# A hybrid attention trunk on one core: another order of layer 0's attention pairs, other stretches of dense work between them, and a second tile for transposed probabilities

## The chip, the cores and the metric

The kernel runs on one core of a Trainium2 chip. The metric is the device time of one execution in microseconds (us), the median of several runs. The engines are TensorE (PE in the profile; its weight loads, which can lie beside its matmuls, are PEld), VectorE (DVE), ScalarE (ACT), GpSimd (POOL) and SyncE (SP, which issues nearly all transfers).

## What is computed

The reference is a decoder trunk of two residual layers, with 512 tokens and a model width of 1024, in float32. Each layer is `x = x + mixer(rmsnorm(x))`, then `x = x + conv_glu_ffn(rmsnorm(x))`. Layer 0's mixer has two groups of eight heads of width 64 that share one input and one output projection:

```python
o_sb = stick_breaking_attention(q, k, v)        # 8 heads
o_nsa = nsa_attention(...)                      # 8 heads, 2 groups of K and V, 3 gated branches
return concatenate([o_sb, o_nsa]) @ w_out
```

A stick-breaking head has `a = exp(log_sigmoid(z) + after)`, where `after` is the sum of `log_sigmoid(-z)` over all later keys up to the query: a running sum along the keys, and no division. A sparse (NSA) head adds three softmax branches, each times its gate: over 31 compressed blocks of keys, over selected blocks, and over a window. With 512 tokens the selected branch and the window branch are plain causal attentions with K and V of their own. Layer 1's mixer has 16 heads of softmax attention with a learned decay.

## The kernel before

**Precision and dense work.** A float32 product with weights is made of three matmuls: activations and weights are both split into a high and a low part (`XH`, `XL`; `whi`, `wlo`), and high by high, high by low and low by high are added up in PSUM. `weights()` (line 177) loads a weight tile and makes its parts, one cast on ACT and one subtraction on DVE. `unit()` (line 197) is one projection of 128 columns: 8 steps of 3 matmuls of 512 columns. `vgroup()` (line 210) projects V for four heads (16 steps of 6 narrower matmuls), `proj()` (line 473) is a part of the output projection (4 steps in layer 0, since each half of the heads has its own), `compress()` (line 640) makes the compressed keys or values out of what `c_use()` (line 619) has gathered, and `mid()` (line 755) loads x again. All weights, and the swapped rows of the rotary helper `rope()` (line 518), are loaded by SP, one after the other. These are generators; `Fill` (line 35) holds them in one queue and `step(n)` runs n steps of it, `get()` runs steps until a named result is there.

**Attention.** Two heads at a time are a pair (`Pair`, line 358; `SbPair`, line 441). A pair has these parts: `S((3,))`, `S((2,))`, `S((0, 1))` make the scores of query blocks 3, 2, and 0 with 1, in PSUM, and start the softmax (DVE, ACT) or the stick-breaking chain (ACT: abs, exp, ln; DVE: one combined operation, the running sums of line 462, the subtraction of line 463; ACT: exp). `N` scales by the denominator and the gate on POOL (softmax pairs alone). `T(0)` to `T(4)` transpose the probabilities, four 128 by 128 blocks at a time, into one PSUM bank; each is copied by ACT into the tile `ph` (line 426). `V` multiplies by the values, 16 matmuls, into the bank `o`, which is then copied out (line 470). `Cmp` (line 691) is the compressed branch; its `S` and `T` hang on the first pair of two heads, as `extra`. Score tiles have two buffers of two banks each, the bank for transposes and the bank `o` have one each, and `ph` has one buffer.

**Order.** `pipeline()` (line 71) takes one pair per turn: the scores of the newest pair, the transposes of the one before it, and `V` of the one before that. A turn is a list of up to ten parts, and after each part a tenth of the turn's dense steps is run:

```python
seq: S(3)+S(2) | V | T(0) | N(2) | T(1) | S(0,1) | T(2) | N(0) | T(3) | T(4)
pairs = [four SbPair] + [h for p in range(4) for h in nsa_pairs(p)]
pipeline(pairs, fl, lambda n: 28 if n < 4 else 6)
```

So layer 0 (line 495) has first four stick-breaking turns with 28 dense steps each, then eight sparse turns (selected and window branch of four pairs of heads) with 6 steps each, and two turns without scores. The dense queue of layer 0 has 163 steps. Layer 1 (line 822) calls the same `pipeline()` with eight pairs and 22 steps a turn. The order in which an engine gets its instructions is fixed when the program is built: the order of the calls is the priority, and an instruction that is planned to have its inputs late lets others of its engine go first. On the chip every engine then takes them in that fixed order.

**Last steps of layer 0.** The output projection's first half (`part`, line 752) needs the outputs of pairs 0 to 3 and goes into the dense queue; the second half (line 763) needs all pairs and comes last, followed by the next norm.

Of the kernel before, what the change touches and what calls it, by code (L numbers as in the profile page):

```python
# [9 lines left out]
F32 = mybir.dt.float32  # L10
# [7 lines left out]
P = 128  # L18
# [13 lines left out]
NPERM = [0, 4, 1, 5, 2, 6, 3, 7]  # L32

# [37 lines left out]
def pipeline(pairs, fill, steps):  # L71

    p1 = p2 = None
    for n, h in enumerate(list(pairs) + [None, None]):
        seq = []
        if h is not None:
            seq.append(lambda: (h.S((3,)), h.S((2,))))
        if p2 is not None:
            seq.append(p2.V)
        if p1 is not None:  # L80
            seq.append(lambda: p1.T(0))
        if h is not None:
            seq.append(lambda: h.N(2))
        if p1 is not None:
            seq.append(lambda: p1.T(1))
        if h is not None:
            seq.append(lambda: h.S((0, 1)))
        if p1 is not None:
            seq.append(lambda: p1.T(2))
        if h is not None:  # L90
            seq.append(lambda: h.N(0))
        if p1 is not None:
            seq += [lambda: p1.T(3), lambda: p1.T(4)]
        f = steps(n)
        done = 0
        for m, a in enumerate(seq):
            a()
            want = f * (m + 1) // len(seq)
            fill.step(want - done)
            done = want  # L100
        p2, p1 = p1, h
# [3 lines left out]
def trunk(ctx, tc, A):  # L105
# [51 lines left out]
    maskb = cp.tile([P, 2, 2, P], BF, name="maskb")  # L157
# [5 lines left out]
    def load_consts():  # L163
        for t, n in ((ones, "ones"), (ident, "ident"), (mask32, "mask2"), (mk, "mk"), (conv, "conv")):
            sp.dma_start(t, A[n])
        pool.tensor_copy(maskb, mask32)

    def warm():

        z = cp.tile([P, SEQ], BF, name="zero")  # L170
# [95 lines left out]
    def finish(fp, src, oh, ol):  # L266
# [20 lines left out]
        def square(m, b, ps):  # L287

            t, w = parts[b], width[b]
            added.append(dve.tensor_add(X[m][:, t], X[m][:, t], ps[:, 0:w]).ins)  # L290
            sq = wp.tile([P, SEQ], F32, tag="sq2", bufs=4, name="sq")
            act.activation(sq[:, 0:w], X[m][:, t], AF.Square)
            return sq[:, 0:w]
# [64 lines left out]
    class Pair:  # L358

# [32 lines left out]
        def S(self, ii):  # L392
            ps = self.scores(ii, None)
            for i in reversed(ii):
                w = P * (i + 1)
                o = EOFF[i] - EOFF[ii[0]]
                for hd in range(2):
                    ei = self.e[:, hd, EOFF[i]:EOFF[i] + w]
                    nm, dn = self.nm[:, hd, i:i + 1], self.dn[:, hd, i:i + 1]
                    add = mk[:, 384 - P * i:512] if self.bias is None else self.bias[:, hd, EOFF[i]:EOFF[i] + w]  # L400
                    dve.tensor_tensor_reduce(ei, ps[:, hd, o:o + w], add, scale=-1.0, scalar=3.0e38,  # L401
                                             op0=ALU.add, op1=ALU.min, accum_out=nm)
                    act.activation(ei, ei, AF.Exp, bias=nm, scale=-1.0, accum_out=dn)  # L403
            if self.extra is not None and 0 in ii:
                self.extra.S()
# [12 lines left out]
        def T(self, n):  # L418
            if n == 0:
                self.ph = self.ap.tile([P, 2560], F32, tag="ph", bufs=1, name="ph")  # L420
            ps = pp.tile([P, SEQ], F32, tag="t", bufs=1, name="t")
            for hd, j in TGRP[n]:
                for i in range(j, NB):
                    o = POFF[hd][j] - 512 * n + (i - j) * P
                    pe.transpose(ps[:, o:o + P], self.e[:, hd, EOFF[i] + j * P:EOFF[i] + j * P + P], ident)  # L425
            act.copy(self.ph[:, 512 * n:512 * n + 512], ps)  # L426
            if self.extra is not None and n == 4:
                self.extra.T()
# [12 lines left out]
    class SbPair(Pair):  # L441


        def S(self, ii):
            def more(ps, r, i):
                for n in range(2):
                    mm(ps[:, i * P:i * P + P], maskb[r, 0, n], maskb[r, 1, n], False, n == 1)
# [47 lines left out]
    def layer0():  # L495
        with ExitStack() as es:
# [8 lines left out]
            def o_tiles(c):  # L505

                if c >= 4 and c % 2 == 0:
# [10 lines left out]
            def rope(f):  # L518
# [5 lines left out]
                u = ap.tile([P, SEQ], F32, tag="rp", bufs=1, name="rp")  # L524
                dve.tensor_mul(u, s, rs)
                dve.tensor_mul(f, f, rc)
                dve.tensor_add(f, f, u)
# [9 lines left out]
            def k_use(key, rp):  # L537
                def use(ps):
                    f = evac(qp, ps, 1.0, "k", 3)
# [5 lines left out]
            def v_use(key, j):  # L545
                def use(tb, ps):
# [4 lines left out]
                    act.activation(gates[:, tb, 8 * j:8 * j + 8], ps[:, 256:264], AF.Exp, scale=nrt[:, tb:tb + 1])  # L551
                    if tb == NB - 1:
                        VT[key] = VT["new"]
                return use
# [38 lines left out]
            def early_bank():  # L593

                if not early:
# [5 lines left out]
                   vgroup(wv(0), 264, v_use(0, 0), v_sp))  # L601
            fl._start(2)
            load_consts()
# [15 lines left out]
            def c_use(key):  # L619
                def use(ps):  # L620
                    f = evac(qp, ps, 1.0, "k", 3)
# [105 lines left out]
            def nsa_pairs(p):  # L727
# [10 lines left out]
                for b, key in ((1, "s"), (2, "w")):  # L738
# [10 lines left out]
            pairs = [SbPair(ap, lambda p=p: fl.get(Q, p), lambda p=p: fl.get(K, p), lambda p=p: fl.get(VT, p // 2),  # L749
                            2 * (p % 2), new_o, True, True, done=pair_done(p)) for p in range(4)]  # L750
            pairs += [h for p in range(4) for h in nsa_pairs(p)]
            part = lambda m: proj(m, [(A["wo0"][m][:, 0:4], 4)], OH[:4], OL[:4], ready=lambda: 3 in OF)
            nq = lambda p: unit(U[8 + p], q_use(("n", p), True))

            def mid():
                make_gates()
# [3 lines left out]
            fl.add(nq(1), mid(), part(0), part(1), nq(2), part(2), part(3), nq(3), part(4), part(5), part(6), part(7))  # L760
            pipeline(pairs, fl, lambda n: 28 if n < 4 else 6)
# [233 lines left out]
def layout(inp):  # L995
# [11 lines left out]
    for n, v in enumerate((sv[:, :256], sv[:, 256:], np.concatenate([vsl, vwn], 1))):  # L1007
        a[f"wv0_{n}"] = _vg(np.concatenate([v, g[:, 8 * n:8 * n + 8]], 1))
    wo = i["ev_w_out"][0].reshape(16, 64, D)
    a["wo0"] = _units(wo[list(range(8)) + [8 + h for h in NPERM]].reshape(D, D))  # L1010
# [32 lines left out]
```

## Time and profile before

| | us |
|---|---|
| median of 3 runs | 1291.14 |
| lowest and highest run | 1289.74, 1291.53 |
| the profiled execution | 1291.93 |
| its span, first to last instruction | 1290.1 |
| TensorE busy in the span | 1271.2 (99%) |
| weight loads busy | 1002.1 (78%) |
| VectorE, ScalarE, GpSimd busy | 693.7, 555.7, 147.9 |

The profile is that of one execution. Matmuls are pipelined and their ends are modelled, so a TensorE that is shown busy need not be at its peak: a start that comes late is often counted to the instruction before it. The chain that ended last is followed back from the last instruction to what released each; a piece of it lasts from its start to that of the next.

### The profile page before, as it was taken

To read this page: it belongs to the slowest core of one execution; us is meant where nothing else is said; L and a number is where in the kernel's file an instruction comes from. 1 tells how busy PE (TensorE), PEld (TensorE's weight loads), DVE (VectorE), ACT (ScalarE), POOL (GpSimd) and SP (SyncE) were. 2 spreads that over 40 slices of the span, in tenths; PEclk is the share of its full clock that TensorE was granted. 3 is DMA by queue.
4 is the path that set the end of the run, shared out by engine and by line. 5 is a ranking of instruction groups with operands and counts; after the bars stand their busy time and mean duration, and the time that the engine had idled before them with its cause. 6 is when DMAs were issued, how large, how long until landed. Compare 5 with 4: busy or idle time off the path is not lost.

```text
span 1290.1 us, 16521 instructions
## 1 busy us (share of the span) xinstructions
PE 1271.2 (99%) x6338; PEld 1002.1 (78%) x6338; DVE 693.7 (54%) x1142; ACT 555.7 (43%) x948; POOL 147.9 (11%) x206
## 2 busy tenths in 40 slices
PE   8999999999999999999999999999999999999997
PEld 5876856567888888888888877866788888888886
DVE  7468665538655434565443443344755543556534
ACT  6556465645433223334342554444533322333442
POOL 0000042223000000000111433321200000000010
PEclk9999999999999999999999999999999999999999
DMA  6315201003333233232344453411333223333232
GB/s 224 95 59 147 87 21 42 19 26 123 98 99 94 78 106 107 92 98 89 94 127 141 145 151 92 120 51 51 122 98 98 88 90 100 108 94 94 88 99 90
DMA packets 50639, 124.00 MB, mean 96 GB/s; under 512 B 6320, under 2 KB 15792, under 8 KB 50560
## 3 DMA queue, kind: packets, MB, share of 16 engines
q1 hardware_dynamic: 49040, 121.35, 31.0%
q10 hardware_dynamic: 1520, 1.59, 0.4%
q8 instruction: 50, 0.82, 0.3%
q14 instruction: 29, 0.24, 0.1%
HBM read 119.28 MB, written 2.13 MB: 94 GB/s over the span
## 4 chain that ended last, share of the span: by engine, by line
PE 93%; DVE 3%; ACT 2%; issue 1%; DMA 1%; SPq 0%; DVEq 0%; ACTq 0%
PE mm L115 80%; PE s L115 6%; PE o L115 4%; PE t L425 3%; DVE e L462 1%; DVE wlo L194 0%; ACT whi L193 0%; DMA x<-x 0%; ACT xh L248 0%; DMA wraw<-wu 0%; DVE lt L457 0%; DVE acc L239 0%; ACT lt L454 0%; DVE e L463 0%; DVE e L401 0%
## 5 line engine op out<-in xcount | busy, mean ns | idle before, releaser
L115 PE MATMUL mm<-xh,whi 128*128 128x512 f32 x936 | 372.2, 398 | 0.9 <-ACT xh L248 0.6
L115 PE MATMUL mm<-xh,wlo 128*128 128x512 f32 x936 | 365.1, 390 | 1.6 <-DVE wlo L194 1.6
L115 PE MATMUL mm<-xl,whi 128*128 128x512 f32 x936 | 365.5, 391 | 0.1
L193 ACT CAST whi<-wraw 128x1024 fp32r<-128x1024 f32 (+2 forms) x219 | 200.0, 914 | 383.5 <-PE mm L115 362.7
L194 DVE TENSOR_TENSOR wlo<-wraw,whi 128x1024 fp32r<-128x1024 f32 (+2 forms) x219 | 236.4, 1079 | 137.4 <-ACT whi L193 134.7
L115 PEld LDWEIGHTS mm<-xh,whi 128*128 128x128 f32 x936 | 175.8, 188 | 44.8 <-issue 8.8
L115 PEld LDWEIGHTS mm<-xl,whi 128*128 128x128 f32 x936 | 175.8, 188 | 40.0 <-DVE xl L249 1.8
L115 PEld LDWEIGHTS mm<-xh,wlo 128*128 128x128 f32 x936 | 176.1, 188 | 37.0 <-DVE wlo L194 2.2
L115 PE MATMUL mm<-gh,whi 128*128 128x512 f32 (+2 forms) x352 | 135.0, 383 | 0.0
L115 PE MATMUL mm<-gl,whi 128*128 128x512 f32 (+2 forms) x352 | 134.8, 383 | 0.0
L115 PE MATMUL mm<-gh,wlo 128*128 128x512 f32 (+2 forms) x352 | 134.8, 383 | 0.0
L416 POOL TENSOR_SCALAR e<-e,dn 128x512 f32<-128x512 f32 (+3 forms) x128 | 78.1, 629 | 176.9 <-DVE dn L410 83.9
L403 ACT ACTIVATE e<-e,nm 128x512 f32<-128x512 f32 (+3 forms) x128 | 70.4, 551 | 50.2 <-DVE nm L401 50.2
L426 ACT COPY ph<-t 128x512 f32<-128x512 f32 x100 | 58.1, 581 | 69.6 <-PE t L425 69.4
L783 DVE TENSOR_TENSOR a<-mm,rstd 128x512 f32<-128x512 f32 x44 | 30.4, 691 | 92.1 <-PE mm L115 91.9
L237 POOL COPY acc<-sq 128x512 f32<-128x512 f32 x4 | 2.8, 706 | 651.4 <-ACT sq L234 651.4
L489 DVE TENSOR_TENSOR x<-x,mm 128x512 f32<-128x512 f32 x62 | 42.6, 686 | 64.2 <-PE mm L115 63.9
L115 PEld LDWEIGHTS mm<-gh,wlo 128*128 128x128 f32 x352 | 66.1, 188 | 13.0
L115 PEld LDWEIGHTS mm<-gl,whi 128*128 128x128 f32 x352 | 66.1, 188 | 12.8
L115 PEld LDWEIGHTS mm<-gh,whi 128*128 128x128 f32 x352 | 66.1, 188 | 12.8
L791 DVE TENSOR_TENSOR b<-mm,rstd 128x512 f32<-128x512 f32 x44 | 30.4, 692 | 72.4 <-PE mm L115 72.3
L787 ACT ACTIVATE tt<-tt 128x512 f32<-128x512 f32 x44 | 27.8, 632 | 86.8 <-DVE tt L786 86.8
(167 smaller groups left out, 1644.3 us busy)
## 6 DMA issues: line engine op xcount, KB each, us to landing
wraw<-wfi SPq DMA_DIRECT2D x88, 512.0 KB
wraw<-wu SPq DMA_DIRECT2D x31, 512.0 KB
wraw<-wfo SPq DMA_DIRECT2D x32, 384.0 KB
wraw<-wfo SPq DMA_DIRECT2D x32, 320.0 KB
wraw<-wo SPq DMA_DIRECT2D x32, 256.0 KB
cb<-cd SPq DMA_DIRECT2D x8, 512.0 KB
x<-x SPq DMA_DIRECT2D x14, 256.0 KB
wraw<-wv SPq DMA_DIRECT2D x6, 528.0 KB
```

The lines of the kernel that those rows point to most:

```text
L115: pe.matmul(out, l, r, start=st, stop=sp_)
L193: act.copy(h, w)
L194: dve.tensor_sub(l, w, h.bitcast(F32))
L403: act.activation(ei, ei, AF.Exp, bias=nm, scale=-1.0, accum_out=dn)
L416: pool.tensor_scalar(ei, ei, self.dn[:, hd, i:i + 1], 1.0, op0=ALU.mult, op1=ALU.mult)
L425: pe.transpose(ps[:, o:o + P], self.e[:, hd, EOFF[i] + j * P:EOFF[i] + j * P + P], ident)
L426: act.copy(self.ph[:, 512 * n:512 * n + 512], ps)
L462: dve.tensor_tensor_scan(ei[:, ::-1], li[:, ::-1], li[:, ::-1], 0.0, op0=ALU.add, op1=ALU.bypass)
L489: dve.tensor_add(X[m], X[m], ps)
L783: dve.tensor_mul(a, ps, rstd)
L787: silu.append(act.activation(t, t, AF.Silu).ins)
L791: dve.tensor_mul(b, ps, rstd)
```

## The change

The parts of a turn get another order: `V` comes right behind `S((0, 1))`, `T(0)` right behind the first scores. The dense steps of a turn go into five stretches, each behind a transpose (six where the newest pair is a stick-breaking one), in place of ten. The compressed branch's scores and transposes become entries of their own. Layer 0's pairs now go in the order stick-breaking, stick-breaking, two sparse, stick-breaking, two sparse, stick-breaking, four sparse. The dense queue is reordered to suit, and each turn has its own number of steps. `ph` gets a second buffer in both layers. The output projection's rows are reordered (`CORD`), so that its first half needs pairs 0, 1, 4 and 2.

```diff
+CORD = [0, 1, 4, 2, 5, 3, 6, 7]
...
+        s = [lambda: (h.S((3,)), h.S((2,))), lambda: h.N(2), lambda: (h.S((0, 1)), h.N(0))] if h is not None else [None] * 3
+        t = [lambda k=k: p1.T(k) for k in range(5)] if p1 is not None else [None] * 5
+        v = p2.V if p2 is not None else None
+        xs = h.extra.S if h is not None and h.extra is not None else None
+        xt = p1.extra.T if p1 is not None and p1.extra is not None else None
+        if h is not None and h.slow:
+            seq = [s[0], t[0], "fill", t[1], "fill", s[2], v, "fill", t[2], "fill", t[3], "fill", t[4], "fill", xt]
+        else:
+            seq = [s[0], t[0], "fill", s[1], s[2], v, t[1], "fill", xs, t[2], "fill", t[3], "fill", t[4], "fill", xt]
+        f, nf, done, m = steps(n), seq.count("fill"), 0, 0
+        for a in seq:
+            if a == "fill":
+                m += 1
+                want = f * m // nf
+                fill.step(want - done)
+                done = want
+            elif a is not None:
+                a()
...
-                self.ph = self.ap.tile([P, 2560], F32, tag="ph", bufs=1, name="ph")
+                self.ph = self.ap.tile([P, 2560], F32, tag="ph", bufs=2, name="ph")
...
     class SbPair(Pair):
+        slow = True
...
-            fl.add(*qk(2), vgroup(wv(1), 264, v_use(1, 1), v_own), *qk(3),
-                   unit(U[12], c_use("k")), unit(U[13], c_use("v")), unit(U[8], q_use(("n", 0), True)),
-                   unit(U[14], k_use("s", True)), compress("k"), compress("v"),
-                   unit(U[15], k_use("w", True)), vgroup(wv(2), 264, v_use("n", 2), v_own))
...
-            part = lambda m: proj(m, [(A["wo0"][m][:, 0:4], 4)], OH[:4], OL[:4], ready=lambda: 3 in OF)
...
+            pairs = [sb[0], sb[1], *nsa[0], sb[2], *nsa[1], sb[3], *nsa[2], *nsa[3]]
+            part = lambda m: proj(m, [(A["wo0"][m][:, 0:4], 4)], OH[:4], OL[:4], ready=lambda: all(c in OF for c in CORD[:4]))
...
-            fl.add(nq(1), mid(), part(0), part(1), nq(2), part(2), part(3), nq(3), part(4), part(5), part(6), part(7))
-            pipeline(pairs, fl, lambda n: 28 if n < 4 else 6)
+            fl.add(unit(U[12], c_use("k")), nq(0), unit(U[14], k_use("s", True, "ks")), unit(U[13], c_use("v")),
+                   compress("k"), vgroup(wv(2), 280, v_use("n"), v_own), compress("v"),
+                   unit(U[15], k_use("w", True, "kw")), *qk(2), nq(1), mid(), vgroup(wv(1), 256, v_use(1), v_own),
+                   *qk(3), nq(2), part(0), nq(3), *[part(m) for m in range(1, NK)])
+            pipeline(pairs, fl, lambda n: (30, 30, 10, 10, 10, 12, 14, 8, 6, 8, 6, 6, 7, 7)[n])
```

To make room for the second `ph`: the rotary helper `rope` multiplies in place and loses its tile `rp`; the tag `k` goes from three buffers to two, and the keys of the selected and the window branch get tags of their own (`ks`, `kw`); the zeros of the warm-up matmuls, the bfloat16 mask and the squares of the last norm move to other pools. The 24 gate columns, before in three groups of 8 beside V's columns (264 wide each), are all with the sparse V (256, 256 and 280 wide), and the gates are made there.

## Rows read from the trace of the kernel before

**Rows 1.** The page's first part: busy time of each engine, share, instructions.

```profile
PE 1271.2 (99%) x6338; PEld 1002.1 (78%) x6338; DVE 693.7 (54%) x1142; ACT 555.7 (43%) x948; POOL 147.9 (11%) x206
```

**Rows 2.** Windows: stretch, length, busy PE, PEld, DVE, ACT, POOL, clock, DMA share, GB/s.

```profile
160.00:288.50 128.50, 128.01 (x692) 76.92 (x690) 71.24 (x232) 74.32 (x197) 38.06 (x66) 1.00 0.10 30
746.00:884.00 138.00, 138.00 (x805) 103.66 (x804) 58.65 (x150) 66.88 (x160) 43.72 (x66) 1.00 0.35 98
```

**Rows 3.** Chain of waits in one turn of layer 1: start, length, piece, instructions.

```profile
792.44 1.70 PE s L115 x8
794.15 1.59 PE mm L115 x6
795.74 2.31 PE o L115 x16
...
799.63 0.44 PE t L425 x4
800.07 2.77 PE mm L115 x12
...
805.35 0.86 PE s L115 x8
```

**Rows 4.** Lines by form, PE, stretch 160 to 288.5: count, busy and mean, idle.

```profile
L425 PE MATMUL t<-ident,e 128*128 128x128 f32 x180 | 28.6, 281 | 0.0
L115 PE MATMUL o<-ph,vt 128*64 128x512 f32 x40 | 16.1, 618 | 0.0
L115 PE MATMUL mm<-oh,whi 128*128 128x512 f32 x32 | 13.6, 425 | 0.0
...
L115 PE MATMUL s<-k,q 64*128 64x512 f32 x32 | 11.3, 641 | 0.0
...
L115 PE MATMUL mm<-xh,whi 128*128 128x512 f32 x18 | 7.9, 438 | 0.0
...
L115 PE MATMUL s<-bd,q 128*128 128x64 f32 x32 | 4.4, 281 | 0.0
...
L115 PE MATMUL mm<-o,whi 128*128 128x512 f32 x12 | 4.2, 408 | 0.0
...
L115 PE MATMUL mm<-o,wlo 128*128 128x512 f32 x6 | 2.5, 408 | 0.0
```

**Rows 5.** Chain of waits in one sparse turn of layer 0.

```profile
228.98 1.00 PE o L115 x2
...
231.04 0.59 PE t L425 x4
...
233.06 1.00 PE o L115 x3
...
234.50 1.44 PE o L115 x9
```

**Rows 6.** Timeline of PE at the two compressions (keys, then values).

```profile
121.71 2.08 PE L115 MATMUL mm<-gt,wc 128*64 128x62 f32 x32
...
128.28 3.19 PE L115 MATMUL mm<-wc,gt 128*62 128x64 f32 x32 [2.04 <-DVE wlo L194]
```

**Rows 7.** A window of 1 us behind that idle time: PE busy, clock, DMA.

```profile
129.00:130.00 1.00, 1.00 (x13) 0.50 0.09 18
```

**Rows 8.** Timeline of PE at the end of layer 0's pairs.

```profile
289.19 0.50 PE L115 MATMUL mm<-o,whi 128*128 128x512 f32 x1 [0.68 <-ACT o L470]
...
291.49 0.46 PE L115 MATMUL mm<-o,whi 128*128 128x512 f32 x1 [0.63 <-DVE x L489]
```

**Rows 9.** Chain of waits: both score pieces of one stick-breaking pair.

```profile
97.47 1.99 PE s L115 x16
...
112.68 1.13 PE s L115 x16
```

**Rows 10.** Timeline of DVE, then of ACT, at the same pair's chain.

```profile
108.64 1.19 DVE L463 TENSOR_TENSOR e<-s,e 128x1024 f32<-128x1024 f32 x1
...
122.60 0.84 ACT L464 ACTIVATE e<-e 128x768 f32<-128x768 f32 x1 [1.59 <-DVE e L463]
```

More of the change, by code (lines that the diff above doesn't have):

```diff
@@ L74, in pipeline @@
     for n, h in enumerate(list(pairs) + [None, None]):
[L75 to L100, printed above, removed]
+        s = [lambda: (h.S((3,)), h.S((2,))), lambda: h.N(2), lambda: (h.S((0, 1)), h.N(0))] if h is not None else [None] * 3
[16 more added lines that the diff above has]
+                a()
         p2, p1 = p1, h
@@ L358, in trunk @@
     class Pair:
+        slow = False
         def __init__(self, ap, q, k, vt, vh, get_o, first, last, bias=None, gate=None, extra=None, done=None):
@@ L426, in T @@
             act.copy(self.ph[:, 512 * n:512 * n + 512], ps)
-            if self.extra is not None and n == 4:
-                self.extra.T()
         def V(self):
@@ L744, in layer0 @@
             qk = lambda p: (unit(U[p], q_use(p, False)), unit(U[4 + p], k_use(p, False)))
-            fl.add(*qk(2), vgroup(wv(1), 264, v_use(1, 1), v_own), *qk(3),
-                   unit(U[12], c_use("k")), unit(U[13], c_use("v")), unit(U[8], q_use(("n", 0), True)),
-                   unit(U[14], k_use("s", True)), compress("k"), compress("v"),
-                   unit(U[15], k_use("w", True)), vgroup(wv(2), 264, v_use("n", 2), v_own))
-            pairs = [SbPair(ap, lambda p=p: fl.get(Q, p), lambda p=p: fl.get(K, p), lambda p=p: fl.get(VT, p // 2),
-                            2 * (p % 2), new_o, True, True, done=pair_done(p)) for p in range(4)]
-            pairs += [h for p in range(4) for h in nsa_pairs(p)]
-            part = lambda m: proj(m, [(A["wo0"][m][:, 0:4], 4)], OH[:4], OL[:4], ready=lambda: 3 in OF)
-            nq = lambda p: unit(U[8 + p], q_use(("n", p), True))
+            nq = lambda p: unit(U[8 + p], q_use(("n", p), True))
+            sb = [SbPair(ap, lambda p=p: fl.get(Q, p), lambda p=p: fl.get(K, p), lambda p=p: fl.get(VT, p // 2),
+                         2 * (p % 2), new_o, True, True, done=pair_done(p)) for p in range(4)]
+            nsa = [nsa_pairs(p) for p in range(4)]
+            pairs = [sb[0], sb[1], *nsa[0], sb[2], *nsa[1], sb[3], *nsa[2], *nsa[3]]
+            part = lambda m: proj(m, [(A["wo0"][m][:, 0:4], 4)], OH[:4], OL[:4], ready=lambda: all(c in OF for c in CORD[:4]))
             def mid():
-                make_gates()
                 load_x()
@@ L1006, in layout @@
     a["wu0"] = _units(np.concatenate([sq, sk, nq, kc, vc, ksl, kwn], 1))
-    for n, v in enumerate((sv[:, :256], sv[:, 256:], np.concatenate([vsl, vwn], 1))):
-        a[f"wv0_{n}"] = _vg(np.concatenate([v, g[:, 8 * n:8 * n + 8]], 1))
+    for n, v in enumerate((sv[:, :256], sv[:, 256:], np.concatenate([vsl, vwn, g], 1))):
+        a[f"wv0_{n}"] = _vg(v)
     wo = i["ev_w_out"][0].reshape(16, 64, D)
-    a["wo0"] = _units(wo[list(range(8)) + [8 + h for h in NPERM]].reshape(D, D))
+    wo = wo[list(range(8)) + [8 + h for h in NPERM]].reshape(NK, P, D)
+    a["wo0"] = _units(wo[CORD].reshape(D, D))
     for n, key in (("k", "ev_cmp_pos_k"), ("v", "ev_cmp_pos_v")):
```

38 lines of the change are left out of this document (20 added, 18 removed).

## The prediction

> **What bounds the kernel.** The page comes first. TensorE is busy for 99% of the span [rows 1], so DVE and ACT matter only where TensorE waits for them. But a busy TensorE may be slow, so the windows come next. In the stretch of layer 0's sparse pairs TensorE is idle for 128.50 - 128.01 = 0.49 us, and its weight loads fill 76.92 of 128.50 us, 60%; in layer 1's pairs it is never idle and the loads fill 103.66 of 138.00 us, 75% [rows 2]. So there is something to find that is not idle time. The chain shows what. In layer 1 the attention parts go in whole runs with dense matmuls between: the four score pieces of S(3) and S(2) take 1.70, V 2.31, S(0,1) 0.86, a transpose group 0.44 us, and twelve dense matmuls 2.77 [rows 3]. In a sparse turn of layer 0, V is in three pieces of 1.00, 1.00 and 1.44 = 3.44 us, and a transpose group with scores or V on both sides takes 0.59 [rows 5]. Those pieces are 1.13 and 0.15 us dearer than the whole ones.
>
> How much that is in all comes from counting the stretch's instructions [rows 4] at layer 1's prices [rows 3]. Transposes: 180 / 4 = 45 groups x 0.44 = 19.8. V: 40 of its widest matmuls, 4 a pair, so 10 x 2.31 = 23.1. Scores: 32 / 4 = 8 pairs x (1.70 + 0.86) = 20.5. Dense: 3 x 32 + 3 x 18 + 12 + 6 = 168 matmuls; twelve in a row take 0.231 each, six behind a score run 1.59 / 6 = 0.265 [rows 3]; I take 0.24, so 40.3. The compressed branch: scores 4.4 [rows 4], four transpose groups 1.8, and by the code eight matmuls at 0.24 = 1.9; together 8.1. The sum is 111.8 us, and the stretch is 128.5: **16.7 us** dearer than layer 1's manner of working, of which 16.2 with a busy TensorE.
>
> The Trainium skill (Perfetto Trace Analysis, Identifying the Most-Contended Engine) says that matmul busy time does not show TensorE's headroom, and that the share of weight loads does. The trace agrees that 99% hides something. By that rule alone, at layer 1's 75%, the stretch would shrink to an estimated 76.92 / 0.751 = 102 us, 26 us less; the count by forms leaves 16.7, since the mix of forms differs, and I go by the count.
>
> **The change, part by part.** The sum is made against the profiled execution, 1291.9 us, 0.8 above the median of the runs shown.
>
> (a) *Whole runs in layer 0's sparse turns.* S(0,1) and V are now one run, V waits for transposes of a turn ago, and the second `ph` lets T(0) write before V has read. Dense steps stand only behind transposes, where they cover the copy that frees the single bank. Steps a stretch: turns 2, 3, 5 and 6 (sparse) have 10, 10, 12 and 14 steps, 2 to 2.8 in each of five; layer 1 has 2.2 in each of ten and shows whole runs. Turns 8 to 11 have 6 or 8, 1.2 to 1.6, against 0.6 before. Half of the sparse turns should thus get back all of their share, 8.1 us, the others a quarter, 1.9: **-10**. Ends: 0 (pieces remain as in [rows 5]) and -16.2.
>
> (b) *The wait at the compressed values.* Before them TensorE is idle for 2.04 us, then at clock 0.50, the lower of its two levels, 1.2 GHz [rows 7]; the 32 matmuls take 3.19 where those of the keys took 2.08 [rows 6], 1.1 more. In the new queue 16 V steps lie between the two compressions, so the gathering on DVE has time: **-3.1**, ends 0 and -3.1.
>
> (c) *The end of the pairs.* TensorE waits 0.68 us for the copy of the last `o` and 0.63 for a DVE result [rows 8], since the dense queue of 163 steps ran dry (28 x 4 + 6 x 8 = 160 by turn 11, the rest in turn 12). The new list sums to 164, and behind the last V still come 6 of its last 7 steps. The first wait is covered, the second in half: **-1.0**, ends 0 and -1.3.
>
> (d) *Layer 1* uses the same turn. The six matmuls between S and V cost 1.59 us where six of a longer run cost 2.77 / 2 = 1.39 [rows 3]; that place is gone: 8 x 0.2 = **-1.6**, ends 0 and, with the two like places that transposes now take, -4.8. The second-to-last turns have no dense steps left in either kernel.
>
> (e) *Stick-breaking turns with few steps.* Before, all four had 28 dense steps to hide a long chain. One pair shows it: scores at 97.47; the subtraction on DVE that frees their first buffer ends at 108.64 + 1.19 = 109.83, 12.4 us later; S(0,1) at 112.68, and the last exp ends at 123.44, 10.8 us later [rows 9, 10]. Now turns 4 and 7 have 10 and 8 steps. By the calls, S(0,1) of turn 4 comes after 1.99 + 2 x 0.44 + 3 steps of 0.72 (three matmuls) = 5.0 us, 7.4 too early. What can go first is V, 2.31, and the other seven steps, 5.0: enough, if the order built for TensorE lets them through, at the price of a less even rest of the turn. Nothing before shows this; the nearest row is the wait of 2.04 in the stick-breaking stretch [rows 6], so I take 2.5 a turn: **+5**, ends 0 and the price of the slower rival below.
>
> *At nothing:* the V widths (264 x 3 and 256 + 256 + 280 are the same columns); the gate exps (12 of 8 columns become 4 of 24, on ACT, behind V's copy); the moved pools. Moved with the reordered queue are their SP transfers: each rotary unit issues four swaps that wait on SP for DVE, with the next weights behind them, and the gathering six; no matmul of [rows 4] names a transfer as what ended its wait, and the cover is the weight pair loaded ahead. If that is gone, a unit's matmuls come late as in [rows 6]. Two `k` buffers in place of three: the gathered keys wait for S(0,1) of pair 0, which is done in the stretch before the queue starts. The positions hold: turns 2 and 3 need the first 58 queued steps, and 60 are done by then, turn 4 needs 74 of 80, turn 7 115 of 116; the first `part` is step 124, behind the V of pair 4 in turn 6.
>
> Sum: -10 - 3.1 - 1.0 - 1.6 + 5 = -10.7; 1291.9 - 10.7 = **1281.2 us**.
>
> **The rivals.** *Full recovery.* All sparse turns run like layer 1 and the chains are hidden: -16.2 - 3.1 - 1.3 - 1.6 = -22.2, 1269.7 us. For it: the program order now has the runs whole. Against: 1.2 steps are 0.86 us, and at the end of the list the queue is thin. The 26 us of the page's rule lie past this end, and I give them nothing of their own beyond this case.
>
> *The order doesn't change in kind.* Engines get their order from planned readiness, not from the calls: [rows 5] has V in three pieces although it is called as one. If the plan splits it again, (a) is 0, and -3.1 - 1.0 - 1.6 + 5 leaves 1291.2: no change.
>
> *Slower: TensorE waits in order at the two early stick-breaking turns.* If S(0,1) of turns 4 and 7 stands in TensorE's order ahead of the work that could cover it, everything behind it waits. Price: 7.4 us in each; then the first transpose of the next turn needs the last exp, 10.8 us behind S(0,1), while V, three transposes, seven steps and the next scores are 2.31 + 1.32 + 5.0 + 1.70 = 10.3: 0.5 more, and with six steps 1.2. That is 16.5, and 1.1 for the clock after each long wait, as in [rows 6]: 18.7. Next to these turns a quarter of (a) is lost, 2.5. In all -7.5 - 3.1 - 1.0 - 1.6 + 18.7 = +5.5: 1297.4 us. It decides from 16 us of such waits on. For it: the 2.04 us, with dense matmuls behind the waiting one [rows 6]. Against: a plan that knows the chain's length lets V go first. The Trainium skill (TensorE: Matmul & The Clock Gate, Step-by-step: what each phase is for) says that TensorE pulls weight loads ahead but keeps matmuls in program order; by that rule no dense matmul would slip past a waiting one, and the wait of [rows 6] agrees.
>
> **How the numbers follow.** Forecast 0.55; full recovery 0.12; no change 0.15; slower 0.13; a gain of 3 to 6 us, with (a) half of what I take, 0.05. A measurement of this kernel tells about 0.2%, 2.6 us, from no change. So faster 0.72, within it 0.15, slower 0.13. The forecast's own bounds, with (a) from 5 to 16 and (e) from 0 to 8, give 1274 to 1289; taking in the unchanged case and half of full recovery, the range is 1271 to 1292.
>
> **What would show it.** In the changed profile V is one piece of 16 in nearly all turns and transposes take 0.44 us; weight loads in the pair stretch rise above 60%; no clock of 0.50 behind the compressions; no idle time at the last `o`. It would be wrong if S(0,1) or the first transposes of the third and fourth stick-breaking pair stand behind idle time of several us, or if V is still in pieces.

## The result, and the profile after

| | median, us | runs | range, us | profiled execution, us | its span, us |
|---|---|---|---|---|---|
| before | 1290.70 | 4 | 1289.74 to 1291.53 | 1291.93 | 1290.1 |
| after | 1301.82 | 4 | 1301.02 to 1302.48 | 1301.55 | 1299.8 |

The changed kernel is 0.9% slower: ratio 1.0086, 95% interval 1.0069 to 1.0104. The prediction was 1281.2 us in a range of 1271 to 1292, so it is wrong by 20.6 us and in sign. The profiled execution of the kernel before is slower than each of its four runs, so the spans differ by 9.7 us where the medians differ by 11.1.

TensorE's line of the page's first part, of the kernel after, answers to [rows 1]:

```profile
PE 1273.2 (98%) x6338; PEld 1003.1 (77%) x6338; DVE 691.5 (53%) x1142; ACT 552.7 (43%) x940; POOL 140.5 (11%) x206
```

The count of matmuls is the same. To see where the time went, both spans are cut at the same three matmuls, counted from the end of the program: the first of the first feed-forward network, of layer 1 and of the second network. Windows of the kernel after (length, then busy PE, PEld, DVE, ACT, POOL, then clock, DMA share, GB/s):

```profile
0.00:313.81 313.81, 297.53 (x1717) 214.32 (x1718) 197.26 (x402) 179.88 (x349) 50.08 (x88) 0.99 0.28 84
313.81:679.14 365.33, 365.33 (x1588) 298.28 (x1587) 191.18 (x237) 129.33 (x163) 10.32 (x8) 1.00 0.31 96
679.14:926.10 246.96, 245.12 (x1396) 189.71 (x1395) 110.83 (x252) 116.01 (x264) 72.95 (x104) 1.00 0.38 112
926.10:1299.80 373.70, 365.26 (x1643) 300.77 (x1641) 192.28 (x252) 127.51 (x164) 7.18 (x6) 0.99 0.30 93
```

The same windows of the kernel before:

```profile
0.00:313.76 313.76, 303.99 (x1717) 215.08 (x1718) 199.38 (x402) 181.81 (x357) 52.60 (x88) 0.99 0.28 84
313.76:674.10 360.34, 360.21 (x1588) 297.62 (x1587) 190.87 (x237) 129.59 (x163) 10.35 (x8) 1.00 0.31 97
674.10:921.26 247.16, 246.69 (x1396) 189.28 (x1395) 111.49 (x252) 116.49 (x264) 77.82 (x104) 1.00 0.38 112
921.26:1290.10 368.84, 360.33 (x1643) 300.13 (x1641) 191.92 (x252) 127.78 (x164) 7.14 (x6) 0.99 0.31 95
```

Two things are to be seen. **The whole loss of the profiled executions lies in the two feed-forward networks**, 4.99 and 4.86 us, which the change does not touch and where TensorE's idle time does not grow (0.13 and 8.51 us before, 0 and 8.44 after). **Layer 0, which the change is about, comes out even**: its busy time falls by 303.99 - 297.53 = 6.46 us for the same 1717 matmuls, and its idle time rises from 9.77 to 16.28, by 6.51.

*The networks.* Here are four units of 24 matmuls in a row in the first network. Windows of the kernel after:

```profile
325.52:331.09 5.57, 5.57 (x26) 4.52 (x24) 3.98 (x6) 3.02 (x4) 0.00 (x0) 1.00 0.40 137
331.09:336.57 5.48, 5.48 (x26) 4.51 (x24) 3.12 (x4) 1.67 (x2) 0.00 (x0) 1.00 0.22 66
336.57:342.13 5.56, 5.56 (x25) 4.52 (x24) 3.33 (x4) 2.40 (x3) 0.00 (x0) 1.00 0.37 126
342.13:347.62 5.49, 5.49 (x26) 4.51 (x25) 3.12 (x4) 1.68 (x2) 0.00 (x0) 1.00 0.25 63
```

The same units of the kernel before, first and last:

```profile
325.48:330.92 5.44, 5.44 (x26) 4.50 (x24) 3.96 (x6) 2.98 (x4) 0.00 (x0) 1.00 0.41 130
...
341.80:347.24 5.44, 5.44 (x26) 4.51 (x24) 3.12 (x4) 1.68 (x2) 0.00 (x0) 1.00 0.25 78
```

Before, each takes 5.44 us; after, they go in turns, 5.56 or 5.57 and 5.48 or 5.49, as the two slots (rotating buffers) of the split weights do. Nothing waits. What differs is where the slots lie. The last value group is 280 columns wide instead of 264, so a slot of `wraw`, `whi` and `wlo` has grown from 4352 bytes (17 x 256; layer 1's 272-wide group set it) to 4480 (17.5 x 256), and the second slot has moved by half of 256 against the first. With the addresses of the built program beside the matmuls of the trace, the mean step from one full-width matmul to the next is:

```
            moving operand   weights of the     steps   mean step
            mod 256          next, mod 256              ns
before      32               32                 3685    227.2
before      160, 192, 224    32                  257    232 to 233
after       32               32                 1918    227.8
after       32               160                1797    232.6
```

The table has the largest groups. 1797 x (232.6 - 227.2) = 9.7 us, and the 1918 steps at 227.8 add 1918 x 0.6 = 1.2: together 10.9, the loss of the medians. `xh`, `gh` and `gl` lie at 32 modulo 256 in both kernels.

*Layer 0.* Timeline of PE after, in the turn of the second stick-breaking pair (some lines left out):

```profile
76.69 2.08 PE L109 MATMUL mm<-gt,wc 128*64 128x62 f32 x32
...
82.52 0.66 PE L419 MATMUL t<-ident,e 128*128 128x128 f32 x4 [0.68 <-ACT ph L420]
86.59 0.80 PE L109 MATMUL s<-k,q 64*128 64x128 f32 x4 [3.41 <-DVE e L456]
...
88.88 0.60 PE L109 MATMUL mm<-vhi,xh 128*128 128x280 f32 x1 [0.32 <-DVE k L341]
```

S(0,1) waits 3.41 us for the subtraction (L456) that frees a score buffer, and the next value group could not go ahead of it: both banks of dense results are full, of the values to be gathered (evacuated at L341) and of the compressed keys. From within that wait on the granted clock is 0.50, the lower of its two levels. Window of the same kernel:

```profile
84.44:91.26 6.82, 4.35 (x22) 3.57 (x23) 6.50 (x9) 1.90 (x2) 0.00 (x0) 0.50 0.16 37
```

DVE's timeline of the same stretch says why the subtraction is late:

```profile
72.65 0.69 DVE L341 TENSOR_TENSOR ks<-mm,rstd 128x512 f32<-128x512 f32 x1
...
73.85 1.32 DVE L189 TENSOR_TENSOR wlo<-wraw,whi 128x1120 fp32r<-128x1120 f32 x1
79.28 0.69 DVE L518 TENSOR_TENSOR ks<-ks,rc 128x512 f32<-128x512 f32 x1 [4.10 <-DMA swp<-ks]
...
80.49 1.22 DVE L450 SCALAR_TENSOR_TENSOR lt<-s,lt 128x1024 f32<-128x1024 f32 x1
...
82.22 2.33 DVE L455 TENSOR_TENSOR_SCAN e<-lt 128x512 f32<-128x512 f32 x2
...
85.32 1.21 DVE L456 TENSOR_TENSOR e<-s,e 128x1024 f32<-128x1024 f32 x1
...
88.16 0.66 DVE L341 TENSOR_TENSOR k<-mm,rstd 128x512 f32<-128x512 f32 x1
```

DVE stands 4.10 us on the rotary swap of the selected keys, and the pair's chain (L450 to L456) and both evacuations are queued behind. ACT had the chain's input ready 2.7 us before DVE took it at 80.49, at 76.72 + 1.05 = 77.77:

```profile
76.72 1.05 ACT L449 ACTIVATE lt<-lt 128x1024 f32<-128x1024 f32 x1
```

Before, DVE stood 3.09 us on such a swap, that of the window keys, with the 96 matmuls of a value group, some 12 us, at hand for TensorE around it and no chain's input ready behind it, and it cost nothing. DVE's row of the kernel before:

```profile
146.37 0.69 DVE L525 TENSOR_TENSOR rp<-swp,rs 128x512 f32<-128x512 f32 x1 [3.09 <-DMA swp<-k]
```

The other new waits of over 0.9 us, PE's timeline after: at the first stick-breaking pair, around the third (158 to 163), at the fourth, and in layer 1's first turn:

```profile
57.76 0.49 PE L109 MATMUL s<-k,q 64*128 64x128 f32 x4 [1.44 <-DVE e L456]
...
158.68 0.65 PE L419 MATMUL t<-ident,e 128*128 128x128 f32 x4 [0.96 <-ACT ph L420]
...
163.35 0.92 PE L109 MATMUL s<-ks,q 64*128 64x384 f32 x4 [0.98 <-DVE e L456]
...
211.18 0.66 PE L419 MATMUL t<-ident,e 128*128 128x128 f32 x4 [1.26 <-ACT ph L420]
...
719.14 0.71 PE L109 MATMUL s<-k,q 64*128 64x128 f32 x6 [1.55 <-DVE nm L397]
```

### The profile page after: what moved, and what is told of

It is laid out like the page before. It is cut to its first block, busy times and chain, and to the rows that moved or that the text cites. A ratio compares the mean times of both kernels' runs of the same rounds, so it can differ in the third digit from the quotient of the medians.

```text
span 1299.8 us, 16507 instructions
## 1 busy us (share of the span) xinstructions
PE 1273.2 (98%) x6338; PEld 1003.1 (77%) x6338; DVE 691.5 (53%) x1142; ACT 552.7 (43%) x940; POOL 140.5 (11%) x206
## 3 DMA queue, kind: packets, MB, share of 16 engines
HBM read 119.28 MB, written 2.13 MB: 93 GB/s over the span
## 4 chain that ended last, share of the span: by engine, by line
PE 88%; DVE 5%; ACT 3%; DMA 1%; issue 1%; SPq 1%; DVEq 0%; POOL 0%; ACTq 0%
PE mm L109 77%; PE s L109 5%; PE t L419 3%; PE o L109 3%; DVE e L455 2%; DVE lt L450 1%; DMA wraw<-wu 1%; DVE e L456 1%; ACT lt L447 0%; SPq L891 0%; ACT lt L449 0%; ACT e L399 0%; DMA x<-x 0%; DVE e L397 0%; ACT lt L448 0%
## 5 line engine op out<-in xcount | busy, mean ns | idle before, releaser
L410 POOL TENSOR_SCALAR e<-e,dn 128x512 f32<-128x512 f32 (+3 forms) x128 | 72.5, 586 | 139.8 <-DVE dn L404 73.9
L419 PEld LDWEIGHTS t<-ident,e 128*128 128x128 f32 x400 | 44.8, 140 | 34.3 <-ACT ph L420 12.9
```

Of the source, the lines that this page charges most:

```text
L410: pool.tensor_scalar(ei, ei, self.dn[:, hd, i:i + 1], 1.0, op0=ALU.mult, op1=ALU.mult)
```

## The experiments

Two questions: is the offset of the slots what the networks lose by (theory P, against R, the moved pools and the new order), and is DVE's stand what layer 0 loses by (theory D, against B, the two full banks alone)?

**e1: slots of 4352 bytes again.**

```diff
-  vgroup(wv(0), 256, v_use(0), v_sp)          # weights sv[:, :256]
+  vgroup(wv(0), 272, v_use(0), v_sp)          # sv[:, :256] and 16 gate columns
-  vgroup(wv(2), 280, v_use("n"), v_own)       # vsl, vwn, all 24 gate columns
+  vgroup(wv(2), 264, v_use("n"), v_own)       # vsl, vwn, the other 8
```

> The gate columns are split 16 + 8 over the first and the last value group, which become 272, 256 and 264 wide: the same columns in all, and the weight slots are 4352 bytes again, as before the change. Theory P (the 4480-byte slots put every second weight unit at another offset than the activations, and its matmuls take 232 to 233 ns instead of 227): the two feed-forward networks give back 4.9 us each, layer 0 stays at about 314 us up to its feed-forward network, total 1292 us (1290 to 1293.5). Rival R (the moved pools or the new order of instructions make those matmuls slow): 1300 to 1303 us, with steps of 232 ns still in every second unit.

**e2: the kernel before with slots of 4480 bytes.**

```diff
+  full = [shape[0], shape[1], 280] if shape[1:] == [NK // 2, 264] else shape
-  w = wp.tile(shape, F32, tag="wraw", ...)
+  w = wp.tile(full, F32, tag="wraw", ...)[:, :, 0:shape[2]]    # whi, wlo alike
```

> The kernel before, with nothing but its weight slots widened from 4352 to 4480 bytes (the 264-wide groups use the first part of a slot). Theory P: the feed-forward networks become 4.5 to 5 us longer each, total 1299.5 to 1302 us. Rival R: 1290 to 1292 us.

Measured: e1 1291.04 us (1290.16 to 1291.63; ratio to before 1.0006, 0.9997 to 1.0016), e2 1300.84 us (1299.81 to 1301.16; 1.0082, 1.0067 to 1.0097). Windows of both networks, e1:

```profile
313.49:673.83 360.34, 360.21 (x1589) 297.70 (x1587) 190.97 (x237) 129.58 (x163) 10.34 (x8) 1.00 0.30 97
...
920.17:1289.00 368.83, 360.31 (x1643) 300.12 (x1641) 192.34 (x252) 127.67 (x164) 7.17 (x6) 0.99 0.29 95
```

and e2:

```profile
312.56:677.89 365.33, 365.33 (x1589) 298.30 (x1587) 191.08 (x237) 129.39 (x163) 10.33 (x8) 1.00 0.30 96
...
925.31:1299.00 373.69, 365.26 (x1643) 300.79 (x1641) 192.13 (x252) 127.54 (x164) 7.15 (x6) 0.99 0.29 93
```

To within a hundredth of a microsecond the networks take the old time with the old slots and the new time with the new ones, whichever kernel stands around them. R falls. The slots are worth 10 to 11 us, nearly all of the loss of 11.1: e2 takes 10.9 us more than the 1289.98 of the kernel before measured beside it, and e1 is within 1.1 us of it.

**b1: the kernel before, everything 128 bytes further.** Does the place of each count, or the offset between the two?

```diff
-  ng = cp.tile([P, 5, NK], F32, name="ng")
+  ng = cp.tile([P, 9, NK], F32, name="ng")[:, 0:5]
```

> The kernel before with one tile at the start of SBUF 128 bytes longer and unused there, so that every later tile lies 128 bytes further: activations and weights move together. Theory P1 (only the offset of the weights against the activations counts): steps stay at 227 ns, total 1290 to 1292 us. Theory P2 (the place of each by itself counts, an odd multiple of 128 bytes being the dear one): steps of 230 to 233 ns in all units, total 1300 us or more.

Measured: 1289.89 us (1289.10 to 1292.00; 0.9999, 0.9990 to 1.0009). Window of the first network:

```profile
313.92:674.26 360.34, 360.21 (x1588) 297.60 (x1587) 191.08 (x237) 129.62 (x163) 10.34 (x8) 1.00 0.30 97
```

Now both operands lie at 160 modulo 256, and 3682 steps take 227.2 ns. P1: at the two places tried, only the offset of the one against the other counts.

**e5: the three rotary multiplications issued at the next unit's turn** (kernel after).

```diff
-  dve.tensor_mul(f, f, rc); dve.tensor_mul(s, s, rs); dve.tensor_add(f, f, s)
+  late.append(rest)      # the three; called at the start of the next use()
```

> The kernel after, with the three VectorE multiplications of each rotary step issued at the next unit's turn, so that VectorE does not stand 4.1 us on the swap's DMA with the second stick-breaking pair's chain queued behind. Theory D (that stand is what TensorE's 3.4 us at 83 us come from): the idle time there falls below 1 us, no granted clock of 0.5 follows it, and the total is 4 to 6 us less than after, 1296 to 1298. Rival B (both banks of dense results are held by the gathered values and the compressed keys, whose evacuations stand behind the pair's chain): the idle time stays above 2.5 us and the total is within 2 us of after.

Measured: 1300.52 us (1300.33 to 1301.04). **Inconclusive**: engines get their order from planned readiness, and the plan put the multiplications ahead of the chain again; DVE stood 3.48 us, TensorE 2.84. These are the numbers that theory B expected, but the edit did not do what it was for, so they do not speak for B.

**e7: 34 and 26 dense steps in the first two turns** (kernel after).

```diff
-  (30, 30, 10, 10, 10, 12, 14, 8, 6, 8, 6, 6, 7, 7)[n]
+  (34, 26, 10, 10, 10, 12, 14, 8, 6, 8, 6, 6, 7, 7)[n]
```

> The kernel after, with 34 and 26 dense steps for the first two stick-breaking pairs instead of 30 and 30, so that the gathered values and the compressed keys are finished before the second pair's scores. Rival B: the idle time near 83 us is gone, with the clock of 0.5 behind it, total 5 to 7 us less than after, 1295 to 1297. Theory D: an idle time of 2.5 us or more stays in the second pair's turn, total 1300 to 1302.

Measured: 1298.44 us (1298.21 to 1298.78), 3.4 less than after, between what B and D expected. The wait of 3.41 is gone and so is the clock of 0.50, since the full banks are emptied before the pair's chain, and in this order DVE does not stand on that swap either. But others come, one of 2.24 us at 119 and this one, PE's timeline:

```profile
71.23 0.51 PE L109 MATMUL mm<-xh,wlo 128*128 128x512 f32 x1 [2.19 <-DVE wlo L189]
```

So moving steps dodges the wait and does not tell D from B.

**e8: the selected keys' rotary multiplications on GpSimd** (on e1, whose time is the one to compare with).

```diff
-  def rope(f):                       # dve.tensor_mul, tensor_mul, tensor_add
+  def rope(f, eng=dve):              # eng.tensor_mul, tensor_mul, tensor_add
-                        rope(f)
+                        rope(f, pool if tag == "ks" else dve)
```

> The changed kernel with value groups of 272, 256 and 264 columns, and the three rotary multiplications of one unit, the selected keys, on GpSimd in place of VectorE. VectorE then cannot stand in front of the second stick-breaking pair's chain for that swap (the delayed multiplications of the earlier run still stood 3.48 us there, so that run did not test theory D). Theory D: VectorE's chain starts some 2.2 us earlier, TensorE's 2.9 us before the second pair's S(0,1) fall below 1 us, no granted clock of 0.5 follows, total 3 to 6 us less than the 1291.0 of the same kernel without this edit: 1285 to 1288 us. Theory B alone (two full banks of dense results): 2 us or more of the wait stay, 1289.5 to 1292 us.

Measured: **1284.44 us** (1283.18 to 1286.80; ratio to before 0.9963, 0.9950 to 0.9976), 6.6 less than e1 (6.3 when each is set against the kernel before measured beside it). Timeline of DVE:

```profile
77.49 0.69 DVE L341 TENSOR_TENSOR k<-mm,rstd 128x512 f32<-128x512 f32 x1 [1.65 <-PE mm L109]
78.50 1.23 DVE L450 SCALAR_TENSOR_TENSOR lt<-s,lt 128x1024 f32<-128x1024 f32 x1 [0.32 <-ACT lt L449]
79.64 0.20 DVE L650 COPY kc<-mm 64x62 f32<-64x62 f32 x1
79.77 3.37 DVE L455 TENSOR_TENSOR_SCAN e<-lt 128x512 f32<-128x512 f32 x2
```

and of POOL, which stands in DVE's place:

```profile
79.95 2.12 POOL L518 TENSOR_TENSOR ks<-ks,rc 128x512 f32<-128x512 f32 x1 [4.70 <-DMA swp<-ks]
82.02 2.21 POOL L519 TENSOR_TENSOR swp<-swp,rs 128x512 f32<-128x512 f32 x1
84.31 1.29 POOL L520 TENSOR_TENSOR ks<-ks,swp 128x512 f32<-128x512 f32 x1
```

PE's timeline: the S(0,1) that waited 2.87 us in e1 and 3.41 after waits no more.

```profile
85.18 0.49 PE L109 MATMUL s<-k,q 64*128 64x128 f32 x4
```

Windows, of the stretch that had the low clock and of all of layer 0:

```profile
84.44:91.26 6.82, 6.21 (x56) 5.51 (x55) 6.82 (x11) 3.83 (x7) 1.69 (x2) 1.00 0.12 44
...
0.00:307.22 307.22, 294.02 (x1717) 212.35 (x1718) 197.08 (x399) 180.23 (x353) 56.02 (x91) 1.00 0.27 86
```

The chain begins 2.0 us earlier (78.50 against 80.49), the evacuations come ahead of it (77.49 against 88.16), the value group runs and the clock stays at its full level. Layer 0 falls from e1's 313.49 us to 307.22. The total and the missing wait are what D expected. But the edit undid two things: the stand, and the place of the evacuations behind the chain. S(0,1) starts 11.76 us after the pair's first scores, against 13.33 in e1: 1.6 us of e1's wait of 2.87 is the earlier chain, and the rest is covered by the value group, which has its banks. So the stand and the full banks together are shown to cost the 6.3 to 6.6 us. Neither was undone alone, and what the late chain would cost with free banks, or the full banks without the stand, is not shown.

**e10, e11, e12: other ways round the stand.** e10 is e1 with every swap issued from GpSimd's DMA queue, e11 the same with e7's steps, e12 e7's steps with the selected and the window keys' multiplications on GpSimd; all three have the aligned attention outputs of e9 below.

```diff
-  sp.dma_start(s[b:b + 8], f[b + 8:b + 16])
+  pool.dma_start(s[b:b + 8], f[b + 8:b + 16])     # e10, e11; the second swap alike
-  rope(f)
+  rope(f, pool if tag in ("ks", "kw") else dve)   # e12
```

> The changed kernel with value groups of 272, 256 and 264 columns, attention outputs at the offset of the weight slots, and every rotary swap issued from GpSimd's DMA queue in place of SyncE's, where it stands behind weight and residual transfers. Theory D with a late issue as the cause: the swaps land 2 to 3 us earlier, the wait near 83 us falls below 1.5 us, total 1284.5 to 1287.5 us. If the swap's own landing is the slow part: the wait stays near 3 us, 1288.5 to 1290.5 us.

> The kernel of the run with 34 and 26 steps and aligned attention outputs (1285.6 to 1291.8 us, with waits of 2.5 us near 69 and 118 us), and its rotary swaps issued from GpSimd's queue. Late issue as the cause: VectorE's 2.6 us at the swap of the window keys and TensorE's 2.6 us behind it near 118 us fall below 1 us, and the total is 1284 to 1286.5 us. Otherwise it stays at 1286 to 1291 us.

> The kernel of the run with 34 and 26 steps and aligned attention outputs, with the rotary multiplications of the selected and the window keys on GpSimd in place of VectorE. Theory D: the wait near 118 us falls below 1 us, 1284 to 1287 us; the wait near 69 us, which is for the weights' low part behind the first pair's chain, stays. Rival: GpSimd's normalisation of the first sparse pair stands behind these multiplications and the transposes wait for it instead, 1288 us or more.

Measured: 1298.66 us (1296.39 to 1303.25), 1294.36 (1294.28 to 1297.99) and 1288.71 (1287.82 to 1290.83). e10 and e11 are slower than either theory expected, and e12 lies where its rival did. Another queue does not bring the swap earlier (issued at 75.23 us, at 75.34 in e1): it waits for the clearing of `swp` on POOL, and that for DVE's last rotary addition of the unit before. POOL's row of e10, then DVE's:

```profile
74.41 0.53 POOL L514 MEMSET swp<- 128x512 f32 x1 [7.21 <-DVE q L520]
...
79.79 0.69 DVE L518 TENSOR_TENSOR ks<-ks,rc 128x512 f32<-128x512 f32 x1 [4.27 <-DMA swp<-ks]
```

e10 and e11 also wait 2.0 and 2.5 us near 248 us, for the compressed probabilities, where e1 and e9 do not: in e10's trace DVE stands 3.98 us there on another swap, that of a pair's queries (at 247.45), with the probabilities' subtraction queued behind, the same pattern once more. e12 keeps the wait near 71, 2.13 us, that it was expected to keep, and the wait near 120 stays at 1.85, so the window keys' swap was not its only cause: there ACT stands 2.67 us on the DMA of a value group's weights (at 116.28), with the copy that frees the transposes' bank queued behind.

**b2 and b3: one half of the change undone, both on e1.** b2 takes the turns away and keeps the order inside a turn; b3 the reverse.

```diff
-  pairs = [sb[0], sb[1], *nsa[0], sb[2], *nsa[1], sb[3], *nsa[2], *nsa[3]]
+  pairs = [*sb, *nsa[0], *nsa[1], *nsa[2], *nsa[3]]     # b2, with the old dense list
-  seq = [s[0], t[0], "fill", s[1], s[2], v, t[1], ...]
+  seq = [S(3,2), V, T(0), N(2), T(1), S(0,1), T(2), N(0), T(3), T(4)]   # b3, steps spread evenly
```

> The changed kernel with the 272, 256 and 264 wide value groups and the turns undone: all four stick-breaking pairs first, then the sparse pairs, with the dense list and the 28 and 6 steps of the kernel before; the four stretches, the order inside a turn and the second tile of transposed probabilities stay. Theory G (the order inside a turn makes whole runs by itself, a quarter of what the pieces cost with 1.2 steps a stretch, 4 us, and 1.6 in layer 1): 1284 to 1287 us. Theory H (whole runs need the dense steps that the turns bring): 1289 to 1292 us, V still in pieces in most sparse turns.

> The changed kernel with the 272, 256 and 264 wide value groups and the order inside a turn undone: the pairs take turns, but each turn has the order and the evenly spread dense steps of the kernel before. Theory G: V is in pieces again, the sparse turns win nothing and the stick-breaking turns with few steps cost what they cost, 1291 to 1298 us. Theory H (the turns bring the gain, the order inside costs it by its wait at 83 us): that wait is gone and the total is 1284 to 1288 us.

Measured: b2 1288.94 us (1287.57 to 1290.42; 0.9988, 0.9979 to 0.9997), b3 1296.10 (1294.43 to 1297.90; 1.0044, 1.0029 to 1.0059). Windows of layer 0, b2:

```profile
0.00:311.84 311.84, 296.98 (x1717) 213.89 (x1718) 196.65 (x402) 181.01 (x353) 49.54 (x88) 0.99 0.27 85
```

and b3:

```profile
0.00:316.48 316.48, 302.13 (x1718) 215.31 (x1718) 197.76 (x402) 180.37 (x353) 51.62 (x88) 0.99 0.27 84
```

Busy time is 303.99 before, 302.13 with the turns alone, 296.98 with the new order alone: nearly all of the busy time won comes from the order inside a turn, with old lists and 1.2 steps a stretch. The total of b2 lies between the two theories, since it has a wait of its own, 2.64 us at the compressed values, for their weights' DMA. In b3, V is in pieces in about half of the turns and the wait of the second turn stands too (3.24 us, ended by the copy of the compressed keys): it belongs to the turns' list. b3's total is in theory G's range, and theory H, which had the wait gone, falls.

**e9, e13, e14: the attention outputs, and more steps for the thin turns.** e9 is e1 with e7's steps and this, e13 is e8 with this:

```diff
-  m = ap.tile([P, NB, 2], F32, tag="cmx", ...)
+  m = ap.tile([P, NB, 8], F32, tag="cmx", ...)[:, :, 0:2]      # 96 bytes ahead of layer 0's outputs
-  bf = c1.tile([P, 16], F32, name="bf")                        # behind OH and OL
+  bf = c1.tile([P, 32], F32, name="bf")[:, 0:16]               # ahead of them
```

e14 is e13 with `(30, 30, 8, 8, 16, 10, 12, 14, 6, 6, 6, 4, 7, 7)`.

> The changed kernel with three edits: value groups of 272, 256 and 264 columns, 34 and 26 dense steps in the first two turns, and unused bytes ahead of the tiles of attention outputs of both layers, so that these lie at the same offset modulo 256 bytes as the weight slots. From the single runs: 1301.8 - 10.8 (slots) - 3.4 (steps) = 1287.6, and by theory P some 280 matmuls of the output projections give back 5.5 ns each, 1.5 us: 1286 us (1284.5 to 1287.5). If the projections' steps have another cause they stay at 232 to 233 ns and the total is 1287.5 or more.

> The changed kernel with value groups of 272, 256 and 264 columns, the selected keys' rotary multiplications on GpSimd, and the attention outputs of both layers at the offset of the weight slots. Theory P: all steps of full-width dense matmuls at 227 ns, some 280 of them 5.5 ns shorter: 1284.4 - 1.5 = 1282.9 us (1282 to 1284). Without such a cost: 1284 to 1285 us.

> The same kernel with 16 and 14 dense steps in the third and fourth stick-breaking turns in place of 10 and 8, taken from sparse turns (10, 10, 12, 14, 8 and 8 become 8, 8, 10, 12, 6 and 4 or 6). Theory E (these turns wait because they have too little dense work): the waits of 1.1, 1.0 and 1.4 us there fall below 0.5 each and the total is 2 to 3 us less than without, 1280 to 1281. Rival: the sparse turns lose as much by their thinner stretches or by new waits: 1282.5 to 1285 us.

Measured: e9 1289.98 us (1285.64 to 1291.78), e13 **1282.96** (1282.46 to 1283.65; ratio to before 0.9943, 0.9930 to 0.9957), e14 1285.16 (1284.66 to 1287.86; 0.9968, 0.9955 to 0.9980). In e9 and e13 every full-width dense step counted, 3984 and 3996, takes 227.2 ns; e13 is 1.5 us below e8, as worked out, though the intervals of the two overlap; the steps are the firmer sign. e8, with the same slots and the outputs where they were, has 282 steps at 232 to 233, so it is the outputs' place against the weights that counts there, and not that of the slots against each other. e9's median lies above the range expected. It spreads over 6 us as its mean granted clock does: 0.998 in the run of 1285.64, 0.994 in that of 1291.78. In the traced one (0.996) the clock falls to 0.50 behind each of two waits of 2.5 us; by the means, it fell in some executions and not in others. e14 is slower than e13, and theory E falls. PE's timeline of e14 in the fourth stick-breaking turn:

```profile
201.67 0.49 PE L109 MATMUL s<-k,q 64*128 64x128 f32 x4 [1.21 <-DVE e L456]
...
206.52 0.63 PE L419 MATMUL t<-ident,e 128*128 128x128 f32 x4 [1.43 <-ACT ph L420]
```

With 14 steps in place of 8 that turn waits 2.64 us instead of 1.25: S(0,1) now stands ahead of dense steps; whether these could have gone first was not tried. e13 beats both kernels.

## Why the prediction was wrong

**The step that failed first is one sentence under "At nothing": the value widths "are the same columns".** They are the same columns for TensorE, and another slot size for the tiles that every dense matmul of the kernel reads. It cost 9.8 us in the two networks and 10.9 us in all (e2, against the kernel before). The prediction read no network.

**The second is the cover named for the moved transfers.** The prediction priced the late swap as a late unit on TensorE, with the weight pair loaded ahead as cover. The swap is waited for by DVE. The trace of before shows such a stand (at 146.37), but on DVE and outside the stretch of TensorE's [rows 4] that the prediction went by. The rotary unit of the selected keys came to stand in the second stick-breaking turn, with a pair's chain behind it, and the cover was the dense work at hand while DVE stood: full banks took it away. Together that cost 6.3 to 6.6 us (e8 against e1).

The terms, by the rows above:

- (a) whole runs, -10. The busy time of layer 0 fell by 6.46 after, and by 303.99 - 294.02 = 9.97 in e8, which has no low clock in layer 0; of these 9.97 some 1.1 are (b)'s slow compression. So -8 to -9: right in kind, a little short. The reason given was not. The sum made it depend on steps a stretch, and b2 has most of it with the 1.2 steps to which a quarter was given. Nor is V one piece "in nearly all turns": it is whole for 8 of 12 pairs after, for 7 before. Counted from the start of each matmul to that of the next, 4.5 us of the 9.97 come from the scores, 2.6 from V and 1.2 from the transposes.
- (b) the compressed values, -3.1. Right: the row below has no idle time ahead of it and 2.02 us in place of the 3.19 of [rows 6]. But 1.1 of it was the low clock of the one execution that was read: e2, with a wait of 2.23 us at the same place, keeps the full clock there. PE's timeline after:

```profile
102.96 2.02 PE L109 MATMUL mm<-wc,gt 128*62 128x64 f32 x32
```

- (c) the end of the pairs, -1.0. Right: both waits of [rows 8] are gone; the dense matmuls follow the last V at once, and V is whole. PE's timeline after:

```profile
280.34 2.37 PE L109 MATMUL o<-ph,vt 128*64 128x512 f32 x16
282.64 0.51 PE L109 MATMUL mm<-oh,whi 128*128 128x512 f32 x1
```

- (d) layer 1, -1.6. The busy time fell by 246.69 - 245.12 = 1.57, as worked out. The 1.55 us that S(0,1) waits in the first turn, at 719.14, took it back: by the code one stretch of five now stands ahead of it there, where half of the turn's dense steps did.
- (e) thin stick-breaking turns, +5. Measured 0.96 + 0.98 + 1.26 = 3.20, in the range given. e14, with more steps and a longer wait in the fourth turn, says that their count is not all that sets it.
- The first two stick-breaking turns stood nowhere in the sum. They kept about their steps (30 for 28), and so were taken as unchanged; they cost the 1.44 us at 57.76 and the second failure.

The slower rival had the right mechanism in the wrong turn: work that could cover a chain stands behind it, in turn 1 and not in 4 and 7. The Trainium skill's rule cited there (TensorE: Matmul & The Clock Gate, Step-by-step: what each phase is for), that matmuls keep program order, agrees with the row at 86.59; the dense group behind it was also held by its bank. The lower of the forecast's own bounds does not follow from its terms: with (a) at 16 and (e) at 0 they give 1270.2, not 1274.

With both failures undone (e8), the change is worth 1284.44 - 1289.69 = -5.3 us, against the -10.7 of the sum. In the profiled executions it is 1284.34 - 1291.93 = -7.6: the sum started from an execution of before that was slow by the clock of [rows 7]. Of the other 3.1 us, 2.6 lie in layer 0. There busy time fell by 9.97 us, where (a) and the slow part of (b) had 11.1, and idle time rose by 13.20 - 9.77 = 3.43, where the waits of (b), (c) and (e) had 5 - 2.0 - 1.0 = 2.0; the first turn's wait, 1.50 in e8, stood in no term. Layer 1 won 0.95 us, where (d) had 1.6.

## What to carry to other kernels

When an edit changes the largest shape of a rotating buffer, compare its slot size before and after, and the time of stages that the edit does not touch: here 128 bytes more in each slot cost more than the whole reordering won. Of an instruction that waits for a DMA on a shared engine, ask what is queued behind it and what TensorE has left to do meanwhile, not only whether its own result is late. Judge an order by busy and by idle time apart; a busy gain of 6.5 us was hidden by an idle loss of the same size.

## What the runs showed of the hardware

- A full-width matmul (128 x 512, the split float32 halves) whose moving operand has the same address modulo 256 bytes as the weights of the next matmul takes 227.2 ns to the next, in the mean of 3685 steps before; with offsets of 128 to 192 bytes between the two it takes 232 to 233, 2.4% more. Moving both together by 128 bytes changes nothing (b1). Smaller offsets occur only in the output projections, with few steps: after, 32 bytes (68 steps, 233.3 ns) and 64 bytes (13 steps, 233.8). No reason was found. The Trainium skill (SBUF — State Buffer, SBUF: two separate sides) gives weight loads a read port of their own and says that TensorE never waits on anyone there. By that alone the two addresses would not matter to each other; the 10.9 us of e2 say that they do, and whether the cost lies in these reads no run here shows.
- While GpSimd multiplied, DVE's two scans took 3.37 us (e8) where they took 2.33 after, and GpSimd's own multiplications 2.12 and 2.21 us, against 1.29 for the addition behind them and 1.28 for each of the two in e12 (at 115.46 and 116.70), where DVE was idle for most of that time. The Trainium skill (same page and section) says that GpSimd and a DVE instruction with two SBUF inputs exclude each other on a shared port; these rows agree in that each is longer beside the other, and do not show how the port is shared.
